# Hybrid RWKV-7 and sparse-attention block on one core: order of the Gram products, layout of the Gram matrices in DRAM, place of the first branch's weight split

## Chip, cores and metric

One core of one Trainium2 chip. The metric is the device time of one execution in microseconds; the time before is the median of three runs. TensorE is PE here (PEld: its weight loads), VectorE DVE, ScalarE ACT, GpSimd POOL, SyncE SP, as in the profile.

## The reference

The kernel computes one block of a model for a sequence of 2048 positions and width 1024. What matters for the change, cut to its core:

```python
p = h @ w_in[l]                       # h: rms_norm(x), scaled and shifted; then a token shift on some columns
(pr, pk, pv, pwd, pad_, z_a, q, ckv, z_b, qi, ki, wi, g_a, g_b) = jnp.split(p, split_at, axis=-1)
y_a = rwkv7_branch(pr, pk, pv, pwd, pad_, ...)      # 8 heads of 64, a scan over the sequence:
#   sa    = einsum('bhvk,bhk->bhv', state, a_t)
#   state = state * w_t + sa b_t + v_t k_t ;  y_t = einsum('bhvk,bhk->bhv', state, r_t)
y_b = dsa_branch(q, ckv, qi, ki, wi, ...)           # 256 keys chosen for each query, softmax over them
br_a = (y_a * jax.nn.silu(z_a)) @ w_pa[l]
br_b = (y_b * jax.nn.silu(z_b)) @ w_pb[l]
merged = jax.nn.sigmoid(g_a) * br_a + jax.nn.sigmoid(g_b) * br_b
x = x + gate * (merged @ w_o[l])
```

## The kernel before, in words

The sequence is cut into four blocks of 512 positions (`tb`, NTB = 4), and the block's stages are written one after the other in `build`. A scheduler orders the instructions of each engine by a priority that `band(p)` sets (a lower number comes first) and by what each instruction waits for; so stages with different bands run beside each other. Tiles come from pools, and a pool opened where an older one lay waits for the last readers of the older one's tiles. fp32 numbers that need full precision are split into a high and a low part, and a product is three matmuls: high-high, high-low, low-high.

1. Selection of keys (to about 800 us), then the projection `h @ w_in` in pieces: `gemm_half` (matmuls at L251, weights loaded at L230 into `wraw`, split into `whi` and `wlo` on ACT and POOL). For z and g, one unit of 128 rows is copied from PSUM into a tile `eo` (L347) and stored to DRAM (L349). The last piece is `gemm_half((2, 3), ("z", "g"))` at band 70000, which ends near 1694 us.
2. Beside the projection, the scan in a chunked form, for each `tb`. `rwkv_pass` (L612) builds, for each of four pairs of heads `p` and 8 chunks `c`, products of `bk` and `ar`, both 128 rows: two heads of 64. Its Gram products (L703) take rows 0 to 63 or 64 to 127 (`hh`) of `bk` and `ar`, 128 x 128 each, four chunks to a PSUM tile `pg`; DVE multiplies the tile with a mask into `gt` (L705), and a DMA stores it to `gmd` (L706). `rwkv_inv` (L722) loads the 32 x 32 diagonal blocks of the stored matrices as `ln` (L730), with one (chunk, head) matrix to a partition, and inverts the triangular matrices by 31 pairs of DVE instructions (`prd` L740, `tm` L742). `rwkv_chain` (L749) goes through the chunks in order: it loads `gmc` (L762), and its matmuls (L777, L782, L788, L791, L797, L801, L808) depend on each other and on the chunk before.
3. `branch_a` (L1122), at band 75000: `split_weights` (L1007) loads the four row blocks of w_pa, casts the high part on ACT (L1019) and subtracts the low part on DVE and POOL in turn (L1020). Then, for 8 steps of 256 positions (`fb`), `gated` (L1024) loads z and y (`zy`, L1057 and L1058; one buffer for y) in two halves and makes `uh`, `ul` of y silu(z) on POOL (L1043), DVE (L1049) and ACT (L1050); `branch` (L1099) does the matmuls (L1111), loads g (L1114), takes its sigmoid, multiplies, and the result goes back to DRAM.
4. Attention (from 1817 us) and the finish (from 2250 us) with the second branch and w_o.

All DMAs below are issued by SP, in the order in which they stand on its queue; an issue whose data isn't ready holds up what stands behind it.

Of the kernel before, what the change touches and what calls it, by code (L numbers as in the profile page):

```python
# [24 lines left out]
FT = mybir.dt.float32  # L25
# [4 lines left out]
OP = mybir.AluOpType  # L30
AX = mybir.AxisListType.X
PSUM = bass.MemoryType.PSUM
# [5 lines left out]
NTB = S // TB  # L38
# [3 lines left out]
FB = 256  # L42
# [9 lines left out]
class Block:  # L52
# [479 lines left out]
    def rwkv_open(self, ctx):  # L532
        nc, x = self.nc, self.x
        V, A, G, DMA = nc.vector, nc.scalar, nc.gpsimd, nc.sync
        R = self.R = {}
# [55 lines left out]
        for i in range(2):  # L591
            h = c1.tile([128, 4, 128], FT, name=f"H{i}")
# [1 line left out]
            R["H"].append(h)  # L594
        R["n"], R["late"] = 0, []
        d = self.d
        R["gm"] = [d.tile([8, 128, 8, 128], FT, name=f"gmd{i}") for i in range(NTB)]
        R["ar"] = [d.tile([8, 128, 4, 128], FT, name=f"ard{i}") for i in range(NTB)]
        R["bk"] = [d.tile([8, 128, 512], FT, name=f"bkd{i}") for i in range(NTB)]
        R["vt"] = [d.tile([512, 512], FT, name=f"vtd{i}") for i in range(NTB)]  # L600
# [11 lines left out]
    def rwkv_pass(self, tb):  # L612
        nc, R = self.nc, self.R
        V, A, T, G, DMA = nc.vector, nc.scalar, nc.tensor, nc.gpsimd, nc.sync
        ld, wk, st, ps = R["ld"], R["wk"], R["st"], R["ps"]
        P = self.PJ[tb]
        gm4 = R["k_gm"][:, None, :].to_broadcast([128, 4, 128])

        def pg(shape=(128, 512)):
            return ps.tile(list(shape), FT, name="pg")  # L620
# [23 lines left out]
        for p in range(4):  # L644
# [10 lines left out]
            u = wk.tile([128, 512], FT, name="u")  # L655
# [40 lines left out]
            G.tensor_copy(wl, e65[:, :, 64])  # L696
            DMA.dma_start(self.WL[tb][p], wl)
            for c0 in (0, 4):
                for hh in range(2):
                    r_ = slice(hh * 64, hh * 64 + 64)  # L700
                    pt = pg((128, 4, 128))
                    for j in range(4):
                        T.matmul(pt[:, j], bk[r_, c0 + j, :], ar[r_, c0 + j, :], start=True, stop=True)  # L703
                    gt = st.tile([128, 4, 128], FT, name="gt", bufs=4)
                    V.tensor_tensor(gt, pt, gm4, op=OP.mult)  # L705
                    DMA.dma_start(R["gm"][tb][c0:c0 + 4, :, 2 * p + hh, :].rearrange("c q t -> q c t"), gt)  # L706
            G.tensor_tensor(bk, bk, e65[:, :, 64:65].to_broadcast([128, 8, 128]), op=OP.mult)
            for c0 in (0, 4):
                pt = pg((128, 4, 128))
# [12 lines left out]
    def rwkv_inv(self, tb):  # L722

        nc, R = self.nc, self.R
        V, G, DMA = nc.vector, nc.gpsimd, nc.sync
        st = R["iv"]
        ln = st.tile([128, 32, 32], FT, name="ln", bufs=1)
        for b in range(2):
            for c in range(8):
                DMA.dma_start(ln[b * 64 + c * 8:b * 64 + c * 8 + 8],  # L730
                              R["gm"][tb][c, b * 32:b * 32 + 32, :, b * 32:b * 32 + 32].rearrange("s h t -> h s t"))
        tm = st.tile([128, 32, 32], FT, name="tm", bufs=1)
        G.memset(tm, 0.0)
        G.memset(tm.rearrange("p a b -> p (a b)")[:, ::33], 1.0)
        prd = st.tile([128, 1024], FT, name="prd", bufs=1)

        for s in range(31):
            r, n = 31 - s, s + 1
            v = prd[:, :r * n].rearrange("p (t j) -> p t j", t=r)
            V.tensor_tensor(v, ln[:, s, n:][:, :, None].to_broadcast([128, r, n]),  # L740
                            tm[:, s, 0:n][:, None, :].to_broadcast([128, r, n]), op=OP.mult)
            V.tensor_tensor(tm[:, n:, 0:n], tm[:, n:, 0:n], v, op=OP.add)  # L742
        tt = ln
        V.tensor_copy(tt.rearrange("p s t -> p t s"), tm)
        DMA.dma_start(R["ti"][tb], tm[0:64])
        DMA.dma_start(R["tt"][tb][0], tt[0:64])
        DMA.dma_start(R["tt"][tb][1], tt[64:128])

    def rwkv_chain(self, tb):  # L749
        nc, R = self.nc, self.R  # L750
# [7 lines left out]
        for c in range(8):  # L758
            arc = ch.tile([128, 4, 128], FT, name="arc")
            DMA.dma_start(arc, R["ar"][tb][c])  # L760
            gmc = ch.tile([128, 8, 128], FT, name="gmc")
            DMA.dma_start(gmc, R["gm"][tb][c])  # L762
            bkc = ch.tile([128, 512], FT, name="bkc")
            DMA.dma_start(bkc, R["bk"][tb][c])
            uv = ch.tile([128, 512], FT, name="uv")
# [353 lines left out]
    def rows(self, t, k, qs):  # L1119
        return t[k * 128:(k + 2) * 128, qs].rearrange("(k p) t -> p k t", p=128)  # L1120

    def branch_a(self, fbs):  # L1122

        nc = self.nc
        with ExitStack() as ctx:
            k1 = self.pool("ba1", 1, ctx=ctx)
            w = self.pool("baw", 2, side="right", ctx=ctx)
            ps = self.pool("bap", 2, PSUM, ctx=ctx)
            W = {}
            self.split_weights(W, k1, w, (("w_pa", 4),), (nc.vector, nc.gpsimd))  # L1130
            self.ba = []
            for fb in fbs:
                tb, qs = fb // 2, slice((fb % 2) * FB, (fb % 2) * FB + FB)
                u = self.gated(w, ps, fb, 0)
                for m in range(0, 8, 2):
                    g = self.branch(w, ps, fb, 0, m, W["w_pa"], u)
                    self.ba.append(nc.sync.dma_start(self.rows(self.GG[tb], m, qs), g))

    def finish(self):
        nc, tc, x = self.nc, self.tc, self.x  # L1140
# [66 lines left out]
    def build(self, upto="all"):  # L1207
# [65 lines left out]
        hctx.close()  # L1273
        R["ictx"].close()
        R["qctx"].close()
        self.band(70000)
        self.gemm_half((2, 3), ("z", "g"))
        gctx.close()
        k = self.pool("late")
        self.lsum = k.tile([128, NQB, 8], FT, name="lsum")  # L1280
        done = range(S // FB)
        self.ubufs = 2
        self.gbufs = 8
        self.pbufs = 2
        self.ybufs = 1
        self.band(75000)
        actx = ExitStack()
        self.hd0 = self.pool("ath0", 1, ctx=actx)
        self.branch_a(done)
        rctx.close()  # L1290
        self.fiA = self.pool("fia", 1, ctx=actx)
        self.fiW = self.pool("fiw0", 1, ctx=actx)
# [84 lines left out]
```

## Time and profile before

| | before |
|---|---|
| median of 3 runs | 2542.9 us (2539.11 to 2544.07) |
| profiled execution, own time | 2535.82 us |
| its span | 2534.0 us |
| PE busy | 2414.3 us (95%) |
| DVE, ACT, POOL busy | 1615.2 (64%), 1235.3 (49%), 804.8 (32%) us |
| DMA traffic | 415.67 MB, mean 164 GB/s |

The span runs from the first to the last instruction of the profiled execution. Times of the rows below count from its start. Matmuls are pipelined: the rows give the length of one from its start to its modelled end, and the next may start earlier. fp32 matmuls that are not split (the Gram products and the chain) stand as two records each, so a row with x8 is four matmuls.

### The profile page before, as it was taken

What the parts mean: (1) busy time and instruction counts of PE and PEld (TensorE: products, weight loads), DVE (VectorE), ACT (ScalarE), POOL (GpSimd) and SP (SyncE); (2) the same over time, 40 slices, a digit from 0 to 9 for tenths busy, and PEclk for the clock granted to TensorE, in tenths of its full rate; (3) what the DMA queues carried; (4) which work ended last, traced back from release to release, by engine and by line L of the source; (5) the groups of instructions that cost most, each with busy time, mean ns of one, the idle gap of its engine ahead of it and who ended that gap; (6) DMA issues with size and microseconds to landing.
All of it is one profiled execution on the core that took longest, in us unless ns stands there. A gap on an engine that the chain in (4) does not pass through costs nothing.

```text
span 2534.0 us, 44949 instructions
## 1 busy us (share of the span) xinstructions
PE 2414.3 (95%) x16776; PEld 2134.6 (84%) x16776; DVE 1615.2 (64%) x3381; ACT 1235.3 (49%) x2024; POOL 804.8 (32%) x694
## 2 busy tenths in 40 slices
PE   4899999999999999999999999999889999989998
PEld 3687878888888998889888989989779999988887
DVE  6614778776877556654936757344478888876443
ACT  4414646555544424334434333352478888865332
POOL 2411111111121333233333332131255555544332
PEclk9999999999999999999999999999999999999999
DMA  7754223423336556777677769978753343155442
GB/s 248 280 152 125 89 83 92 125 96 96 104 98 217 147 164 193 191 203 225 194 206 212 214 188 276 298 240 250 232 166 87 91 118 99 29 182 192 142 150 71
DMA packets 423496, 415.67 MB, mean 164 GB/s; under 512 B 80010, under 2 KB 339890, under 8 KB 418404
## 3 DMA queue, kind: packets, MB, share of 16 engines
q1 hardware_dynamic: 422692, 404.33, 53.1%
q0 software_dynamic: 576, 8.39, 0.8%
q8 instruction: 132, 2.16, 0.4%
q14 instruction: 96, 0.79, 0.1%
HBM read 254.04 MB, written 160.15 MB: 163 GB/s over the span
## 4 chain that ended last, share of the span: by engine, by line
PE 49%; DMA 7%; DVE 5%; issue 3%; ACT 2%; SPq 2%; POOL 2%; POOLq 0%; ACTq 0%; DVEq 0%
PE g L251 16%; PE fo L1196 6%; PE yv L993 4%; PE br L1111 4%; PE pt L976 3%; PE pg L703 2%; PE lg L959 2%; PE lg L960 2%; DMA xt<-in_w_pb_dram 1%; PE pp L808 1%; PE pp L791 1%; PE zu L797 1%; PE hp L801 1%; PE pp L788 1%; DVE prd L740 1%
## 5 line engine op out<-in xcount | busy, mean ns | idle before, releaser
L251 PE MATMUL g<-hh,whi 128*128 128x256 f32 (+1 forms) x2176 | 718.9, 330 | 8.8 <-DVE eo L265 4.7
L251 PE MATMUL g<-hl,whi 128*128 128x256 f32 (+1 forms) x2176 | 715.3, 329 | 2.9 <-POOL hl L169 2.9
L251 PE MATMUL g<-hh,wlo 128*128 128x256 f32 (+1 forms) x2176 | 714.9, 329 | 1.4 <-POOL wlo L237 1.4
L237 POOL TENSOR_TENSOR wlo<-wraw,whi 128x1024 fp32r<-128x1024 f32 (+1 forms) x89 | 225.1, 2529 | 748.3 <-ACT whi L236 695.0
L251 PEld LDWEIGHTS g<-hh,whi 128*128 128x128 f32 x2176 | 416.0, 191 | 54.7 <-issue 6.5
L251 PEld LDWEIGHTS g<-hl,whi 128*128 128x128 f32 x2176 | 416.2, 191 | 43.4 <-issue 4.1
L251 PEld LDWEIGHTS g<-hh,wlo 128*128 128x128 f32 x2176 | 416.0, 191 | 41.7 <-issue 4.3
L431 DVE SCALAR_TENSOR_TENSOR sc<-re,wi,sc 128x1024 f32<-128x1024 f32 (+7 forms) x154 | 170.7, 1108 | 56.7 <-ACT re L425 50.8
L425 ACT ACTIVATE re<-ixs 128x1024 f32<-128x1024 f32 (+7 forms) x176 | 140.4, 816 | 135.5 <-PE ixs L423 78.7
L236 ACT CAST whi<-wraw 128x1024 fp32r<-128x1024 f32 (+1 forms) x89 | 92.8, 1043 | 174.2 <-PE g L251 132.3
L976 PE MATMUL pt<-ident,lt 128*128 128x128 f32 x1088 | 168.1, 275 | 7.0 <-ACT tp L982 4.3
L966 ACT ACTIVATE lt<-lt,nm 128x128 f32<-128x128 f32 (+15 forms) x128 | 154.8, 1212 | 15.3 <-DVE nm L965 15.2
L987 DVE TENSOR_TENSOR pl<-pt,ph 128x512 fp32r<-128x512 f32 (+1 forms) x216 | 139.0, 657 | 31.6 <-ACT ph L986 30.7
L423 PE MATMUL ixs<-kim,st 128*128 128x512 f32 (+3 forms) x608 | 150.2, 373 | 8.3 <-ACT re L425 4.8
L962 DVE CUSTOM_DVE_ANT_0 lt<-lg,mask 128x512 f32<-128x512 f32 (+3 forms) x256 | 147.4, 589 | 16.5 <-PE lg L960 9.0
L993 PE MATMUL yv<-ph,vp 128*128 128x256 f32 (+1 forms) x576 | 152.1, 285 | 5.7 <-ACT ph L986 5.6
L993 PE MATMUL yv<-pl,vp 128*128 128x256 f32 x576 | 153.0, 301 | 2.0 <-POOL pl L984 1.8
L959 PE MATMUL lg<-m,sq 128*128 128x256 f32 (+3 forms) x384 | 136.6, 365 | 5.9 <-DMA mask<-mask 4.1
L423 PEld LDWEIGHTS ixs<-kim,st 128*128 128x128 f32 x608 | 113.1, 190 | 34.5 <-ACT re L425 6.9
L976 PEld LDWEIGHTS pt<-ident,lt 128*128 128x128 f32 x1088 | 125.7, 141 | 16.9 <-ACT tp L982 5.3
L986 ACT CAST ph<-pt 128x512 fp32r<-128x512 f32 (+1 forms) x216 | 116.4, 564 | 20.8 <-PE pt L976 14.3
L960 PE MATMUL lg<-m,sq 128*128 128x256 f32 (+3 forms) x384 | 126.2, 336 | 0.0
(343 smaller groups left out, 5106.6 us busy)
## 6 DMA issues: line engine op xcount, KB each, us to landing
wraw<-in_w_in_dram SPq DMA_DIRECT2D x88, 512.0 KB
gg<-eo SPq DMA_DIRECT2D x64, 256.0 KB
gmd<-gt SPq DMA_DIRECT2D x64, 256.0 KB
gmc<-gmd SPq DMA_DIRECT2D x32, 512.0 KB
g<-gg SPq DMA_DIRECT2D x64, 256.0 KB
m<-ks SPq DMA_DIRECT2D x32, 512.0 KB
pj<-eo SPq DMA_DIRECT2D x52, 256.0 KB
x<-in_ada_w_dram SPq DMA_DIRECT2D x24, 512.0 KB
```

The costliest lines, as they stand in the source:

```text
L237: nc.gpsimd.tensor_tensor(lo[:, :, :n], raw[:, :, :n], hi[:, :, :n].bitcast(FT), op=OP.subtract)
L251: T.matmul(p[:, s], a[:, k], b[:, k, s], start=n == 0, stop=n == 3 * KD - 1)
L423: T.matmul(p[:, a:b], st[:, h], M[i][:, k0 + a:k0 + b], start=i == 0, stop=i == 1)
L425: A.activation(r[:, :kn], p[:, :kn], AF.Relu)
L431: V.scalar_tensor_tensor(o, r[:, :kn], wi, o, op0=OP.mult, op1=OP.add)
L959: T.matmul(p[:, :kn], sq[:, qb * 128:(qb + 1) * 128], m1[:, k0:k1_], start=True, stop=False)
L960: T.matmul(p[:, :kn], sq[:, qb * 128:(qb + 1) * 128], m2[:, k0:k1_], start=False, stop=True)
L962: V.tensor_tensor_reduce(lt[:, k0:k1_], p[:, :kn], mk, 1.0, -3.0e38, OP.subtract, OP.max, cm[:, i:i + 1])
L966: ex = A.activation(lt[:, :n], lt[:, :n], AF.Exp, bias=nm, accum_out=lsum[:, qb, h:h + 1])
L976: T.transpose(p[:, o:o + 128], L[i][:, kt * 128:(kt + 1) * 128], self.ident)
L993: T.matmul(yv[:, qs], vp[:, kt, :], b[:, o:o + nn], start=kt == 0 and i == 0, stop=kt == last and i == 1, skip_group_check=True)
L1196: T.matmul(p, a[:, k, q], b[:, k, s], start=n == 0, stop=n == 23)
```

## The change

Three things, and the title's last words ("output tiles stay in a bank of their own, passes at 2 tiles") say what is as before.

- In `rwkv_pass`, the two PSUM tiles of the halves are taken together, and the products are written alternating, half 0 and half 1 of chunk `j`, then of `j + 1`; the two evictions and stores follow.
- The Gram matrices lie in DRAM by row: [row, chunk, head, column] in place of [chunk, row, head, column]. A store writes four chunks of a head; `rwkv_inv` loads its blocks by 2 DMAs of 64 partitions in place of 16 of 8; `rwkv_chain` reads `[:, c]`.
- `branch_a` is cut in two. `branch_open` opens the pools of w_pa (`ba1`), of its raw tiles (`bas`) and of the branch's PSUM (`bap`), all on the right side, and splits w_pa; it stands ahead of the last projection piece in `build`, at band 72000. `branch_a` opens the pool for u, z, y and g (`baw`) after the projection and goes through the steps.

```diff
-        R["gm"] = [d.tile([8, 128, 8, 128], FT, name=f"gmd{i}") for i in range(NTB)]
+        R["gm"] = [d.tile([128, 8, 8, 128], FT, name=f"gmd{i}") for i in range(NTB)]
...
             for c0 in (0, 4):
+                pts = [pg((128, 4, 128)) for hh in range(2)]
+                for j in range(4):
+                    for hh in range(2):
+                        r_ = slice(hh * 64, hh * 64 + 64)
+                        T.matmul(pts[hh][:, j], bk[r_, c0 + j, :], ar[r_, c0 + j, :], start=True, stop=True)
                 for hh in range(2):
-                    r_ = slice(hh * 64, hh * 64 + 64)
-                    pt = pg((128, 4, 128))
-                    for j in range(4):
-                        T.matmul(pt[:, j], bk[r_, c0 + j, :], ar[r_, c0 + j, :], start=True, stop=True)
                     gt = st.tile([128, 4, 128], FT, name="gt", bufs=4)
-                    V.tensor_tensor(gt, pt, gm4, op=OP.mult)
-                    DMA.dma_start(R["gm"][tb][c0:c0 + 4, :, 2 * p + hh, :].rearrange("c q t -> q c t"), gt)
+                    V.tensor_tensor(gt, pts[hh], gm4, op=OP.mult)
+                    DMA.dma_start(R["gm"][tb][:, c0:c0 + 4, 2 * p + hh, :], gt)
...
         for b in range(2):
-            for c in range(8):
-                DMA.dma_start(ln[b * 64 + c * 8:b * 64 + c * 8 + 8],
-                              R["gm"][tb][c, b * 32:b * 32 + 32, :, b * 32:b * 32 + 32].rearrange("s h t -> h s t"))
+            b_ = slice(b * 32, b * 32 + 32)
+            DMA.dma_start(ln[b * 64:b * 64 + 64], R["gm"][tb][b_, :, :, b_].rearrange("s c h t -> (c h) s t"))
...
-            DMA.dma_start(gmc, R["gm"][tb][c])
+            DMA.dma_start(gmc, R["gm"][tb][:, c])
...
-    def branch_a(self, fbs):
+    def branch_open(self, ctx):
         nc = self.nc
-        with ExitStack() as ctx:
-            k1 = self.pool("ba1", 1, ctx=ctx)
-            w = self.pool("baw", 2, side="right", ctx=ctx)
-            ps = self.pool("bap", 2, PSUM, ctx=ctx)
-            W = {}
-            self.split_weights(W, k1, w, (("w_pa", 4),), (nc.vector, nc.gpsimd))
...
+        k1 = self.pool("ba1", 1, side="right", ctx=ctx)
+        w = self.pool("bas", 2, side="right", ctx=ctx)
+        ps = self.pool("bap", 2, PSUM, side="right", ctx=ctx)
+        W = {}
+        self.split_weights(W, k1, w, (("w_pa", 4),), (nc.vector, nc.gpsimd))
+        return ps, W["w_pa"]
+
+    def branch_a(self, fbs, ctx, ps, wt):
+        nc = self.nc
+        w = self.pool("baw", 2, side="right", ctx=ctx)
...
+        bctx = ExitStack()
+        self.band(72000)
+        ba = self.branch_open(bctx)
         self.band(70000)
         self.gemm_half((2, 3), ("z", "g"))
...
-        self.branch_a(done)
+        self.branch_a(done, bctx, *ba)
+        bctx.close()
```

What the scheduler makes of it, at three places. A row of the built order gives line, operation, output<-inputs with the number of the buffer, size, and how many alike follow each other.

PE, Gram products of a head pair in one of the passes, among matmuls of the chain (L782 to L791) and of the projection (L251). Before, `pg_13751`, `13759`, `13767` and `13775` are the four tiles of this pair; the second and the third stand next to each other:

```order
L703 MATMUL pg_13751<-ar_13728,bk_13729 128x128 x4
L782 MATMUL zu_14280<-ttc_14264,t1c_14265 32x32 x4
L690 MATMUL pg_13737<-ei_13739,blk_8649 128x512
L782 MATMUL zu_14280<-ttc_14264,t1c_14265 32x32 x4
L788 MATMUL pp_14290<-H0_8664,arc_14256 128x128 x4
L791 MATMUL pp_14290<-uv_14262,gmc_14258 64x64 x6
L703 MATMUL pg_13759<-ar_13728,bk_13729 128x128 x4
L703 MATMUL pg_13767<-ar_13728,bk_13729 128x128 x4
L791 MATMUL pp_14290<-uv_14262,gmc_14258 64x64 x2
```
With the change `pg_13709` and `13710` are the two halves of the first four chunks, `13725` and `13726` those of the others:

```order
L704 MATMUL pg_13709<-ar_13686,bk_13687 128x128 x4
L783 MATMUL zu_14224<-ttc_14208,t1c_14209 32x32 x4
L690 MATMUL pg_13695<-ei_13697,blk_8649 128x512
L783 MATMUL zu_14224<-ttc_14208,t1c_14209 32x32 x4
L789 MATMUL pp_14234<-H0_8664,arc_14200 128x128 x4
L792 MATMUL pp_14234<-uv_14206,gmc_14202 64x64 x6
L704 MATMUL pg_13710<-ar_13686,bk_13687 128x128 x4
L704 MATMUL pg_13725<-ar_13686,bk_13687 128x128 x4
L792 MATMUL pp_14234<-uv_14206,gmc_14202 64x64 x2
```
Each tile's four products still stand in one row, and the two halves of the first four chunks are apart by other work. Over the whole program a row of four of one half and a row of four of the other make a run of eight 8 times now, 7 before.

SP, loads for the first inversion (`ln`), behind the chain's first `gmc`. Before:

```order
L762 DMA gmc_9860<-gmd0_8668 128x1024
L762 DMA gmc_9939<-gmd0_8668 128x1024
L730 DMA ln_9188<-gmd0_8668 8x32x32 x8
L714 DMA bkd0_8676<-gt_9169 128x4x128
L75 DMA lat3_76<-eo_15479 128x512
L714 DMA bkd0_8676<-gt_9177 128x4x128
...
L720 DMA vtd0_8680<-gt_9185 128x4x128
L730 DMA ln_9188<-gmd0_8668 8x32x32 x6
...
L730 DMA ln_9188<-gmd0_8668 8x32x32 x2
L633 DMA pk_9312<-pj1_69 128x512
```
With the change:

```order
L763 DMA gmc_9832<-gmd0_8668 128x1024
L763 DMA gmc_9911<-gmd0_8668 128x1024
L732 DMA ln_9188<-gmd0_8668 64x32x32 x2
L716 DMA bkd0_8676<-gt_9169 128x4x128
L75 DMA lat3_76<-eo_15423 128x512
L716 DMA bkd0_8676<-gt_9177 128x4x128
```
The 16 loads stood in three rows, with stores and loads of other stages between; now both stand in the first row's place.

SP, end of the last projection piece. `gg2`, `gg3` <- `eo` are the stores of its units; `z`, `y`, `g` the loads of the branch's first step. Before, from the fifth-last of these stores on:

```order
L349 DMA gg3_84<-eo_18712 128x512
L1018 DMA xt_18956<-in_w_pa_dram 128x1024
L1018 DMA xt_18960<-in_w_pa_dram 128x1024
L1057 DMA z_18974<-z0_77 128x2x256
L764 DMA bkc_15061<-bkd3_8679 128x512
L762 DMA gmc_15059<-gmd3_8671 128x1024
L766 DMA uv_15063<-vtd3_8683 64x512
L1058 DMA y_18976<-ya0_101 128x2x256
L1057 DMA z_18984<-z0_77 128x2x256
L1114 DMA g_19019<-gg0_81 128x2x256
L849 DMA bo_15135<-bod3_8687 128x2x256
L1114 DMA g_19049<-gg0_81 128x2x256
```
With the change:

```order
L349 DMA gg2_83<-eo_18851 128x512
L349 DMA gg3_84<-eo_18903 128x512
L1058 DMA z_18921<-z0_77 128x2x256
L1059 DMA y_18923<-ya0_101 128x2x256
L1058 DMA z_18931<-z0_77 128x2x256
L1115 DMA g_18966<-gg0_81 128x2x256
L1115 DMA g_18996<-gg0_81 128x2x256
...
L1059 DMA y_18933<-ya0_101 128x2x256
L1115 DMA g_19198<-gg0_81 128x2x256
```
The loads of z, y and g stood among the projection's stores; now the first of them stands directly behind the last two stores, and the second y behind seven loads of g.

## Rows read from the trace of the kernel before

**Rows 1.** The page's first part: busy time (share of the span), instructions.
```profile
PE 2414.3 (95%) x16776; PEld 2134.6 (84%) x16776; DVE 1615.2 (64%) x3381; ACT 1235.3 (49%) x2024; POOL 804.8 (32%) x694
```

**Rows 2.** Busy table: stretch, length, PE, PEld, DVE, ACT, POOL, PEclk, DMA share, GB/s.
```profile
1100.00:1694.00 594.00, 592.56 (x5775) 538.22 (x5775) 334.70 (x604) 226.08 (x383) 183.75 (x180) 1.00 0.78 230
1694.00:1713.00 19.00, 15.88 (x174) 14.37 (x172) 9.95 (x10) 9.28 (x15) 9.90 (x6) 0.91 0.49 145
1740.00:1780.00 40.00, 33.52 (x262) 32.55 (x261) 11.96 (x18) 10.16 (x18) 5.12 (x4) 0.96 1.03 314
1780.00:1817.00 37.00, 34.31 (x280) 33.50 (x281) 13.99 (x21) 10.54 (x19) 5.16 (x4) 1.00 0.59 191
```

**Rows 3.** The same table, beside the first inversion.
```profile
1030.00:1090.00 60.00, 52.09 (x384) 47.71 (x383) 46.88 (x85) 15.39 (x23) 14.01 (x8) 0.94 0.61 162
1083.00:1090.00 7.00, 5.93 (x23) 5.06 (x24) 2.57 (x7) 0.49 (x1) 0.00 (x0) 0.51 0.66 168
```

**Rows 4.** Timeline of PE, Gram matmuls: start, us, engine, line, operation, out<-in, count.
```profile
898.09 1.16 PE L703 MATMUL pg<-ar,bk 64*128 64x128 f32 x8
...
903.29 1.71 PE L703 MATMUL pg<-ar,bk 64*128 64x128 f32 x16
```

**Rows 5.** Timeline of SP's queue, loads of the first inversion.
```profile
1011.44 6.57 SPq L730 DMA_DIRECT2D ln<-gmd  x8
...
1032.22 0.88 SPq L730 DMA_DIRECT2D ln<-gmd  x2
```

**Rows 6.** Timeline of DVE, inversion 0; idle before <-releaser in brackets.
```profile
1037.94 0.19 DVE L740 TENSOR_TENSOR prd<-ln,tm 128x31 f32<-128x31 f32 x1 [5.69 <-DMA pk<-pj]
...
1084.40 0.19 DVE L742 TENSOR_TENSOR tm<-tm,prd 128x31 f32<-128x31 f32 x1
```

**Rows 7.** Timeline of PE around the end of the projection.
```profile
1693.60 0.69 PE L782 MATMUL zu<-ttc,t1c 32*32 32x32 f32 x16
...
1697.76 1.11 PE L797 MATMUL zu<-xx,ttc 64*64 64x64 f32 x16 [1.32 <-issue]
...
1701.03 0.58 PE L1111 MATMUL br<-uh,w_pal 128*128 128x256 f32 x1 [1.28 <-DVE w_pal L1020]
...
1712.10 0.39 PE L1111 MATMUL br<-uh,w_pal 128*128 128x256 f32 x1 [0.37 <-POOL w_pal L1020]
```

**Rows 8.** Groups of instructions, 1693 to 1817 us: the split of w_pa.
```profile
L1020 POOL TENSOR_TENSOR w_pal<-xt,w_pah 128x1024 fp32r<-128x1024 f32 x2 | 5.6, 2788 | 0.2
L1019 ACT CAST w_pah<-xt 128x1024 fp32r<-128x1024 f32 x4 | 4.1, 1044 | 1.9 <-DMA xt<-in_w_pa_dram 1.5 <-DMA gg<-eo 0.3
L1020 DVE TENSOR_TENSOR w_pal<-xt,w_pah 128x1024 fp32r<-128x1024 f32 x2 | 3.2, 1606 | 3.0 <-ACT w_pah L1019 3.0
```

**Rows 9.** Timeline of SP's queue: loads of the first branch.
```profile
1658.84 0.59 SPq L1058 DMA_DIRECT2D y<-ya  x1
1659.47 0.48 SPq L1057 DMA_DIRECT2D z<-z  x1
```

**Rows 10.** Chain that ended last, 1690 to 1720 us: start, us, what.
```profile
1691.20 2.48 PE g L251 x19
...
1693.70 0.59 ACT eo L347
...
1694.31 3.50 DMA gg<-eo
...
1718.36 2.75 DMA g<-gg
```

**Rows 11.** Instruction groups y, z (1693 to 1817 us) and uh (1640 to 1800).
```profile
L1043 POOL TENSOR_TENSOR y<-z,y 128x512 f32<-128x512 f32 x12 | 15.7, 1304 | 86.2 <-DMA y<-ya 46.2 <-DMA z<-z 33.1 <-DVE ul L1051 3.5
...
L1049 DVE TENSOR_TENSOR z<-y,sz 128x512 f32<-128x512 f32 x13 | 10.8, 834 | 30.7 <-POOL y L1043 30.7
...
L1050 ACT CAST uh<-z x15: 601/617/622, 1669.2 to 1799.2; 128x512 fp32r<-128x512 f32 x15
```

**Rows 12.** Timeline of PE, a stop inside the branch.
```profile
1747.93 0.39 PE L1111 MATMUL br<-uh,w_pah 128*128 128x256 f32 x1 [3.92 <-DVE g L1116]
```

More of the change, by code (lines that the diff above doesn't have):

```diff
@@ L1120, in rows @@
         return t[k * 128:(k + 2) * 128, qs].rearrange("(k p) t -> p k t", p=128)
-    def branch_a(self, fbs):
+    def branch_open(self, ctx):
         nc = self.nc
-        with ExitStack() as ctx:
-            k1 = self.pool("ba1", 1, ctx=ctx)
-            w = self.pool("baw", 2, side="right", ctx=ctx)
-            ps = self.pool("bap", 2, PSUM, ctx=ctx)
-            W = {}
-            self.split_weights(W, k1, w, (("w_pa", 4),), (nc.vector, nc.gpsimd))
[L1131 to L1137, printed above, removed]
+        k1 = self.pool("ba1", 1, side="right", ctx=ctx)
[7 more added lines that the diff above has]
+        w = self.pool("baw", 2, side="right", ctx=ctx)
+        self.ba = []
+        for fb in fbs:
+            tb, qs = fb // 2, slice((fb % 2) * FB, (fb % 2) * FB + FB)
+            u = self.gated(w, ps, fb, 0)
+            for m in range(0, 8, 2):
+                g = self.branch(w, ps, fb, 0, m, wt, u)
+                self.ba.append(nc.sync.dma_start(self.rows(self.GG[tb], m, qs), g))
     def finish(self):
@@ L1275, in build @@
         R["qctx"].close()
+        self.ubufs = 2
+        self.gbufs = 8
+        self.pbufs = 2
+        bctx = ExitStack()
+        self.band(72000)
+        ba = self.branch_open(bctx)
         self.band(70000)
@@ L1281, in build @@
         done = range(S // FB)
-        self.ubufs = 2
-        self.gbufs = 8
-        self.pbufs = 2
         self.ybufs = 1
```

## The prediction

> **What bounds the kernel now.** I read the page's busy table first: TensorE is busy 95% of the span, so only what shortens its queue of matmuls, or what it stands idle for, can move the end [rows 1]. The table of stretches then says where it stands idle [rows 2]. From 1100 to 1694 us it is busy 592.56 us of 594.00: there a gain on another engine is worth nothing. There are three stretches that the change touches in which it is not full: 1030 to 1090 us, beside the first inversion; 1694 to 1713 us, where the projection ends and the first branch starts; and 1740 to 1780 us, inside the branch, with the DMA engines at a share of 1.03. In the first the loss is 60.00 - 52.09 = 7.9 us of idle time, and the granted clock is 0.51 over 1083 to 1090 us, the lower of its two levels, which costs about half of 7.00, 3.4 us: 11.3 us together [rows 3]. In the second it is 19.00 - 15.88 = 3.1 us, and the clock is 0.91. Last I read single rows around the three places: TensorE's timeline, SyncE's DMA issues, the chain that ended last.
>
> **Gram products: 0 us.** Each of the 64 groups of four products is 8 records. A group alone takes 1.16 us; two groups of opposite row halves back to back take 1.71 us, not 2.3 [rows 4]: where a product of the upper rows stands next to one of the lower rows, they share time. The rule that speaks of this is in the Trainium skill, "TensorE: Matmul & The Clock Gate", Part 3, on packing small matmuls by row and column tiling: matmuls with few rows that lie in distinct row groups of the array run concurrently. By it the source order of the change (half 0, half 1, half 0, ...) would hide half of all these products; the 1.71 us agree with it. But by the built order the four products of one tile still stand together: almost every row of that table is x4 on one tile, and the two halves are neighbours about as often as before (8 runs of eight against 7). What the source alternates, the order sets back into fours. If full alternation came about, 64 groups would lose half of 1.16 us each where they aren't paired already, 28 us with the 7 or 8 pairs taken off; as the order stands I take 0, -1 to +1.
>
> **Loads of the inversion: -4 us.** Before, 16 DMAs of 8 partitions fetch the blocks. SyncE issues the first 8 from 1011.44 for 6.57 us and the last two at 1032.22 [rows 5]; behind these stands pk. VectorE starts the first product pair at 1037.94, having waited 5.69 us, by the row for pk, and ends the last at 1084.40 [rows 6]: so 46 us of VectorE work, mixed with that of a pass, run through just the stretch in which TensorE loses 11.3 us [rows 3]. With the change one row of two DMAs stands where the first eight stood, and nothing of it is left behind the lat, qs and bkc rows. If two DMAs with as many pieces take what 16 took on SyncE, twice 6.57 = 13.1 us, they end at about 1024.6, and the pairs could start 13 us earlier, into time in which VectorE waits (the 5.69 us among it). Bounds: all 11.3 us gone would be -10 with what remains of the clock, and the pairs only taking the place of the pass's own VectorE work would be up to +4. I take -4, since the pairs' 46 us don't shrink, and the pass's own evictions still wait in the same VectorE queue. The three later inversions lie where TensorE is full (592.56 of 594.00): 0, whichever way. The gmd stores and gmc loads keep their 512-byte and 4-KB pieces; I take 0 for them, under the same cover.
>
> **w_pa split, moved ahead: -3.4 us.** Before, the first cast waits behind the last eo copies on ScalarE, and TensorE stops for the low parts twice, 1.28 us at 1701.03 and 0.37 at 1712.10 [rows 7]; with the clock at 0.91 over 19 us, another 1.7 [rows 2]. Sum -3.35. The work itself is 4 casts of 1.04, 2 VectorE subtractions of 1.6 and 2 GpSimd ones of 2.8 us [rows 8], now beside the last projection, where those engines are not full. Were a cast to stand before an eo copy and wait for its weights, the copy and its g tile would be late: +2 at most. Nothing of the chain late either: -5.
>
> **What the change adds: a wait for z and y at the end of the projection, +10.4 us.** Before, the branch's pool lies on space that is free early: SyncE issues the first y at 1658.84 and the second z at 1659.47 [rows 9], and the first u is cast at 1669.2 [rows 11], 24 us before the last projection matmul ends at 1693.7, where the copy of its tile starts [rows 10]. With w_pa's tiles opened first, that pool comes to lie on the projection's own wlo and eo tiles. The built order shows it: every z, y and g load stands behind the last two gg stores. From T0, the end of the last projection matmul, the chain of waits has in its own rows: eo copy 0.59, store 3.50 to landing, a load of as much as one of these (128x2x256 numbers, 256 KB) 2.75 [rows 10], then GpSimd y 1.30, VectorE z 0.83, ScalarE uh 0.62 [rows 11]; with 0.5 us for two issues that is T0+10.1 for the first branch matmul. Meanwhile TensorE has only the chain's last chunk, six rows from 0.69 us, as at 1693.60, to 1.1, as at 1697.76, 6.0 us in all, with two exposed waits of 1.3 us, as the one of 1.32 there [rows 7]: it ends at T0+8.6, 1.5 us idle. 14 branch matmuls (1.8 us, by 2.48 us for 19 of the same shape [rows 10]) later the second half of u is needed. Its y has one buffer, free at about T0+8.8, and its load stands behind seven g loads: u at about T0+16, 4.2 us idle. Two more windows of the lower clock, as the one after the pause at 1701, cost 1.7 each. Idle and clock 2.6 + 1.5 + 4.2 + 3.4 = 11.7, of which 1.3 is there before: +10.4. Bounds: +3 (the store and the load overlap with the chain's last chunk, the clock holds) to +14 (the seven g loads, 1.8 MB, hold y up by another 4 us).
>
> **The branch without its lead: +4 us.** Each of 8 steps moves 12 DMAs of 256 KB for 96 matmuls. Before, it enters with two u ready and all g loaded, and still stops 3.92 us at 1747.93 [rows 12], with the DMA share at 1.03 [rows 2], while attention's first loads run. With no u in hand each late load shows. Bounds 0 and +10; I take +4, one more stop like that one.
>
> **Sum.** 0 - 4 - 3.4 + 10.4 + 4 = +7.0 us. The profiled execution took 2535.8 us and becomes 2542.8. It stands 7.1 us under the median of the three runs, 2542.9, against which the change is timed: **2550 us** (2549.9 rounded). A difference under 0.2%, 5 us, can't be told from none.
>
> **Rivals.**
> - *The inversion's early start pays in full, faster.* Pairs that start 13 us sooner take all 11.3 us of [rows 3] away, w_pa 3.4, and the switch costs 6 (one clock window, y behind fewer g loads): -8.7, 2534 us. It decides if the pairs come ahead of the pass's evictions, that is if they begin before about 1026. For it: VectorE waits then. Against it: the 46 us of pairs. 0.25.
> - *Nothing to be told.* The switch costs 8, with no lost lead, and the inversion and w_pa give 7 to 8: 2543 us. For it: the branch's DMA share is only 0.59 from 1780 on [rows 2], so a lead can be made up. 0.30.
> - *DMA pile-up.* All 12 loads of the first step (3 MB) come at once behind T0 and meet attention's first loads: the whole +10 of the lost lead and +13.5 at the switch, less 3.5: +20, 2562 us. 0.11.
> - *Halves overlap after all*, as the alternation says it does: -28, 2515 us. The price is from [rows 4], against it stands the built order. 0.03. The Trainium skill's "TensorE: Matmul & The Clock Gate", Part 3, has this as its rule.
> - My forecast: 2550 us, its own range 2548 to 2556. 0.31.
>
> **Numbers.** Under 2537.8 lie the first and the fourth rival: 0.28 faster. The second is 0.30 same. Forecast and pile-up: 0.42 slower. The range is 2533 to 2563: it leaves out the far half of the first rival, the fourth, and the pile-up's far end, some 0.19.
>
> **What would show it.** Gram rows of x8 at 1.16 us, few x16. One row of ln loads near 1011 us, the pairs' start before 1030, and fewer than 11.3 us lost in the 60 us around it. No wait for w_pal. SyncE's first z and y after the last gg store, GpSimd's y waiting for them, TensorE idle 8 to 9 us in the 20 after T0, at the lower clock for one to three windows. I am wrong if z and y are issued some 30 us before T0 still, if the x16 rows come to the most, or if TensorE is full from T0 on.

## The result, and the profile after

| | before | after |
|---|---|---|
| median | 2542.74 us (4 runs) | 2560.15 us (4 runs, 2557.59 to 2561.9) |
| ratio | | 1.0067, 95% interval 1.0045 to 1.0089 |
| span of the profiled execution | 2534.0 us | 2555.8 us |

The change costs 17.4 us by the medians. (Between the two profiled executions it is 21.8 us: that of before lies 6.9 us under its median, that of after 2.6 us.) The prediction said 2550, slower, with a range to 2563. TensorE has the same share, 95%, and is busy 14.2 us longer [rows 1]:

```profile
PE 2428.5 (95%) x16776; PEld 2148.6 (84%) x16776; DVE 1619.7 (63%) x3381; ACT 1233.7 (48%) x2022; POOL 805.6 (32%) x694
```
The busy table of the kernel after (columns as in [rows 2]): beside the first inversion, beside the second, beside the fourth, a piece behind the last projection matmul, and the whole stretch from there to the first matmul of attention.

```profile
1030.00:1090.00 60.00, 57.23 (x497) 53.17 (x496) 50.93 (x91) 19.78 (x31) 21.26 (x16) 1.00 0.72 195
1240.00:1270.00 30.00, 26.69 (x214) 24.66 (x215) 17.21 (x28) 10.30 (x16) 8.14 (x8) 0.89 0.65 173
1583.00:1593.00 10.00, 8.08 (x54) 7.21 (x52) 2.55 (x5) 2.42 (x5) 0.00 (x0) 0.66 1.05 292
1708.60:1729.10 20.50, 13.86 (x64) 12.25 (x65) 10.29 (x19) 13.91 (x21) 4.27 (x4) 0.50 0.70 227
1703.80:1836.50 132.70, 112.20 (x856) 108.19 (x855) 49.66 (x78) 44.79 (x73) 20.55 (x16) 0.88 0.75 231
```
And the row of before for that whole stretch:

```profile
1693.70:1816.45 122.75, 110.47 (x953) 106.98 (x952) 51.58 (x78) 40.71 (x66) 22.76 (x16) 0.97 0.73 226
```
Beside the first inversion only 60.00 - 57.23 = 2.8 us are idle, at the full clock, where 7.9 were [rows 3]; beside the second and the fourth, where TensorE was full, it now stands 3.3 and 1.9 us and the clock is 0.89 and 0.66. The last stretch takes 132.7 us instead of 122.75 and holds fewer matmul records, 856 instead of 953: a chunk of the scan's chain (96 records, some 6.5 us of TensorE in seven rows of 0.7 to 1.2) has come to stand ahead of the projection's end. That end, T0 from here on, comes 10.1 us later (1703.8, 1693.7).

Timeline of PE, rows that answer to [rows 4, 7]: two Gram rows, the waits for the second and the fourth inversion, and the first branch matmuls of the two halves of u.

```profile
899.32 1.16 PE L704 MATMUL pg<-ar,bk 64*128 64x128 f32 x8
...
904.52 1.71 PE L704 MATMUL pg<-ar,bk 64*128 64x128 f32 x16
...
1255.39 1.06 PE L778 MATMUL zu<-t1c,gmc 32*32 32x32 f32 x16 [3.31 <-DMA t1c<-tid]
...
1585.72 1.06 PE L778 MATMUL zu<-t1c,gmc 32*32 32x32 f32 x16 [1.92 <-DMA t1c<-tid]
...
1714.56 0.80 PE L1112 MATMUL br<-uh,w_pah 128*128 128x256 f32 x2 [1.42 <-ACT uh L1051]
...
1722.29 0.80 PE L1112 MATMUL br<-uh,w_pah 128*128 128x256 f32 x2 [4.38 <-ACT uh L1051]
```
Gram rows are as before: x8 in 1.16 us, x16 in 1.71. Timeline of SP's queue, to [rows 5, 9]:

```profile
1013.07 4.32 SPq L732 DMA_DIRECT2D ln<-gmd  x2
...
1694.65 10.11 SPq L349 DMA_DIRECT2D gg<-eo  x2
1706.58 0.37 SPq L1058 DMA_DIRECT2D z<-z  x1
1707.00 0.46 SPq L1059 DMA_DIRECT2D y<-ya  x1
...
1708.02 4.90 SPq L1115 DMA_DIRECT2D g<-gg  x7
1713.88 0.36 SPq L1059 DMA_DIRECT2D y<-ya  x1
```
The ln loads are two DMAs of 4.32 us together. The z, y and g loads come behind the last gg store, for whose tile SP waits from 1694.65 on. DVE and POOL, to [rows 6, 11]: the first instruction of the first inversion, and the first four y products of the branch.

```profile
1021.99 0.19 DVE L741 TENSOR_TENSOR prd<-ln,tm 128x31 f32<-128x31 f32 x1 [3.76 <-DMA ln<-gmd]
```
```profile
1711.86 1.27 POOL L1044 TENSOR_TENSOR y<-z,y 128x512 f32<-128x512 f32 x1 [9.48 <-DMA y<-ya]
1718.83 1.27 POOL L1044 TENSOR_TENSOR y<-z,y 128x512 f32<-128x512 f32 x1 [5.70 <-DMA y<-ya]
1723.85 1.28 POOL L1044 TENSOR_TENSOR y<-z,y 128x512 f32<-128x512 f32 x1 [3.74 <-DMA y<-ya]
1728.65 1.29 POOL L1044 TENSOR_TENSOR y<-z,y 128x512 f32<-128x512 f32 x1 [3.53 <-DMA y<-ya]
```
The waits of PE between the projection and attention, to [rows 12]: engine, line, awaited, us, times, longest.

```profile
PE br L1112 <- ACT uh L1051: 9.6, 3, 4.4
PE br L1112 <- DVE g L1117: 8.2, 5, 2.9
```

### The profile page after: what moved, and what is told of

Its sections match the earlier page's. It is cut to its first block, busy times and chain, and to the rows that moved or that the text cites. A ratio compares the mean times of both kernels' runs of the same rounds, so it can differ in the third digit from the quotient of the medians.

```text
span 2555.8 us, 44911 instructions
## 1 busy us (share of the span) xinstructions
PE 2428.5 (95%) x16776; PEld 2148.6 (84%) x16776; DVE 1619.7 (63%) x3381; ACT 1233.7 (48%) x2022; POOL 805.6 (32%) x694
## 4 chain that ended last, share of the span: by engine, by line
PE 47%; DMA 7%; DVE 6%; issue 3%; ACT 2%; POOL 1%; SPq 1%; POOLq 0%; ACTq 0%; DVEq 0%
PE g L251 13%; PE fo L1202 5%; PE yv L994 4%; PE br L1112 4%; PE pt L977 3%; PE pg L704 2%; PE lg L960 2%; PE lg L961 2%; PE pp L809 1%; PE zu L798 1%; PE pp L792 1%; PE pp L789 1%; DMA xt<-in_w_pb_dram 1%; PE hp L802 1%; DMA g<-gg 1%
## 5 line engine op out<-in xcount | busy, mean ns | idle before, releaser
L251 PE MATMUL g<-hh,whi 128*128 128x256 f32 (+1 forms) x2176 | 719.0, 330 | 4.0 <-DVE prev L339 3.1
L251 PE MATMUL g<-hl,whi 128*128 128x256 f32 (+1 forms) x2176 | 717.6, 330 | 2.9 <-POOL hl L169 2.8
L251 PE MATMUL g<-hh,wlo 128*128 128x256 f32 (+1 forms) x2176 | 715.1, 329 | 1.7 <-POOL wlo L237 1.7
L251 PEld LDWEIGHTS g<-hh,whi 128*128 128x128 f32 x2176 | 417.4, 192 | 47.2 <-issue 5.5
L251 PEld LDWEIGHTS g<-hl,whi 128*128 128x128 f32 x2176 | 417.3, 192 | 44.1 <-POOL hl L169 3.7
L251 PEld LDWEIGHTS g<-hh,wlo 128*128 128x128 f32 x2176 | 417.2, 192 | 41.3 <-issue 4.4
L987 ACT CAST ph<-pt 128x512 fp32r<-128x512 f32 (+1 forms) x216 | 116.1, 564 | 20.9 <-PE pt L977 14.5
```

Source lines behind the costliest of these rows:

```text
L251: T.matmul(p[:, s], a[:, k], b[:, k, s], start=n == 0, stop=n == 3 * KD - 1)
```

## The experiments

Each ratio is to the kernel before, run beside it on the same chip; its medians there were 2540.3 (e1 to e4), 2542.9 (e5 to e8) and 2540.8 us (e9 to e12). "The stretch" is that from the last projection matmul to the first matmul of attention, 122.75 us before and 132.70 after, in one execution of each. T0 itself can't be compared to better than several us between two executions: TensorE's order is the same in e9 and in the changed kernel up to 1722 us, and T0 is 9.3 us apart, most of it from 834 to 869 us.

| run | median us | ratio, 95% interval | the stretch us, its PE records |
|---|---|---|---|
| e1 alternating alone | 2547.5 | 1.0032 (1.0019 to 1.0045) | 126.00, 857 |
| e2 layout alone | 2549.4 | 1.0034 (1.0017 to 1.0051) | 122.70, 856 |
| e11 both of them | 2551.7 | 1.0042 (1.0027 to 1.0056) | 123.10, 856 |
| e3 split ahead alone | 2552.6 | 1.0043 (1.0027 to 1.0058) | 136.30, 953 |
| e4 change, first u ahead | 2544.1 | 1.0015 (1.0001 to 1.0028) | 126.20, 858 |
| e5 alternation forced | 2561.4 | 1.0086 (1.0068 to 1.0103) | 174.80, 1364 |
| e6 chunk ahead | 2552.6 | 1.0046 (1.0032 to 1.0060) | 125.30, 896 |
| e7 split and first u ahead | 2540.5 | 0.9996 (0.9985 to 1.0007) | 127.30, 954 |
| e8 busy in the wait | 2561.5 | 1.0082 (1.0067 to 1.0097) | 132.90, 909 |
| e9 change, two y | 2550.3 | 1.0028 (1.0015 to 1.0041) | 120.00, 858 |
| e10 e7 with two y | 2525.7 | 0.9937 (0.9918 to 0.9957) | 113.30, 953 |
| e12 before, two y | 2536.0 | 0.9976 (0.9965 to 0.9986) | 118.70, 952 |

**The parts alone.** e1 has the first part of the diff (products alternating), e2 the second (layout, ln and gmc loads), e11 both, e3 the third (the split ahead, `baw` behind).

> Only the Gram products written alternating, all else as before. Theory A (the order sets them back into fours, nothing moves): within 5 us of the kernel before, 2538 to 2548 us, and nearly all Gram rows x8 at 1.16 us, some 8 of x16 at 1.71. Rival (both tiles taken together hold the pass up): 5 to 10 us slower, with waits for gt before the Gram products. Rival (halves overlap): 20 to 28 us faster.

> Only the Gram matrices by row and the two ln loads. Theory A (the first inversion starts 16 us earlier and TensorE gains 10 to 12 us there, but inversions 1 and 3 make it wait as in the changed kernel, 5 to 7 us each): within 5 us of before. Rival (the waits at inversions 1 and 3 have to do with the other parts): 8 to 12 us faster. Rival (the layout is what costs the 17 us): 10 to 17 us slower.

The two are slower by much the same, and neither by the expected way: theory A said within 5 us for both. (e1 has the number of its first rival, 5 to 10 us, but not its waits: the Gram products wait 0.9 us for gt in e1 as before.) In both the projection ends about 8 to 10 us later (1701.8 and 1703.3) with the chain one chunk further, and the stretch behind it is no shorter without that chunk. Waits of PE in e1, 1701.8 to 1730 us, and the stretch of both:

```profile
PE br L1112 <- ACT w_pah L1020: 2.3, 2, 1.3
PE br L1112 <- POOL w_pal L1021: 1.5, 1, 1.5
PE br L1112 <- DVE w_pal L1021: 0.9, 2, 0.5
```
```profile
1701.80:1827.80 126.00, 107.28 (x857) 103.27 (x856) 45.95 (x71) 36.71 (x58) 17.89 (x13) 0.95 0.67 210
```
```profile
1703.30:1826.00 122.70, 107.41 (x856) 103.80 (x854) 45.97 (x71) 36.72 (x58) 18.94 (x13) 0.94 0.68 216
```
The waits for the w_pa split, 1.28 and 0.37 us before [rows 7], are 4.7 us in e1 (2.7 in e2): the chunk that stood among the first branch matmuls had covered them. In e2 the waits beside the second and fourth inversions are there as in the changed kernel (3.32 us at 1258, 1.85 at 1588), so they belong to the layout.

> The change without its third part: Gram products alternating and the layout by row, the branch as before. Theory (both alone move the same chunk of the chain ahead of the projection's end, so the loss is had once): 6 to 11 us slower than before. Rival (each part has a loss of its own): 14 to 18 us slower.

As the theory had it, the loss is had once: 0.42%, not 0.66%.

**The chunk by itself.** e6 is the kernel before with one ordering edge:

```diff
+                mark = T.matmul(pp[0:64, ...], gmc[64:128, h, 0:64], uv[64:128, ...], ...)   # chain of tb 3, c == 6
...
+                    if kind == "g" and i == 15 and tb == 3:
+                        with self.tc.issue_after(self.R["mark"].ins):
+                            p = self.unit(wt, tb)
```

> The kernel before, with one ordering edge: the last projection unit's matmuls stand behind the seventh chunk's products with uv in the last chain, so that one chunk of the chain instead of two is left behind the projection, as in the runs with the alternation alone and the layout alone. Nothing else differs. Theory A (those runs were slower because that chunk no longer covers the waits for the w_pa split, and the phase behind the projection does not get shorter without it): 5 to 10 us slower than before. Rival (the place of the chunk is worth nothing, the loss was in the new loads and tiles): within 3 us of before.

It is slower by 0.46%, at least as much as e1 and e2, and waits for the same split, 4.6 us. So chain work that moves ahead of the projection's end is enough for a loss of that size. That isn't all that e6's trace shows: only 57 records leave the stretch, and from attention's first matmul to the last matmul it takes 713.8 us, 707.8 before, which is open. Waits of PE from 1702 to 1732 us, and the stretch:

```profile
PE br L1117 <- ACT w_pah L1025: 2.4, 1, 2.4
PE br L1117 <- POOL w_pal L1026: 2.2, 2, 1.2
```
```profile
1702.00:1827.30 125.30, 109.69 (x896) 105.76 (x894) 49.35 (x74) 38.39 (x61) 21.88 (x16) 0.95 0.68 215
```
**The wait for z and y.**

> Only the split of w_pa ahead of the last projection piece, with the pool of z, y, g and u opened behind it. Theory A (the wait for z and y at the end of the projection, and the lower clock behind it, are the whole of the loss): 14 to 20 us slower than before, first branch matmul 10 to 11 us after the last projection matmul, TensorE at the lower clock for 15 to 25 us there. Rival (the loss needs the other parts too): within 6 us of before.

Slower by 0.43%, 11 to 12 us, between the two and nearer to theory A. The first branch matmul comes 11.65 us after the projection's end, and the stretch is 13.5 us longer than before with the same records:

```profile
1695.50:1831.80 136.30, 120.44 (x953) 116.11 (x951) 51.15 (x82) 46.71 (x78) 21.78 (x18) 0.90 0.72 227
```
e4 gives the first step a pool of its own (14 KB for each partition) beside the w_pa split:

```diff
+        w0 = self.pool("ba0", 1, side="right", ctx=ctx)
+        self.ubufs = self.ybufs = 1
+        self.u0 = self.gated(w0, ps, 0, 0)
...
-            u = self.gated(w, ps, fb, 0)
+            u = self.gated(w, ps, fb, 0) if fb else self.u0
```

> The changed kernel, but z, y and u of the first step in a pool of their own of 14 KB that lies on free space, loaded beside the projection; g and all later steps as in the changed kernel. Theory A (the late z and y of the first step are the cause): TensorE goes on with the branch at once, no wait over 2 us and at most one window of the lower clock in the 30 us behind the last projection matmul; 10 to 16 us faster than the changed kernel, 2544 to 2551 us. Rival (the loads of the later steps and of g, all late, pile up on the DMA engines whatever the first step has): the stop moves to the second step, under 5 us gained, 2555 us or more.

TensorE goes on with the branch at once, and 13 us of the 17 come back. But the stops move on, as the rival had it in part: 2.73, 2.64 and 6.33 us at 1724.66, 1762.59 and 1775.31, and only 6.5 us of the gain lie in the stretch. Behind it e4 is 9.2 us shorter (700.3 us from attention's first matmul to the last matmul, against 709.5), all of it in attention's first 130 us. There a wait of the changed kernel is gone:

```profile
PE lg L960 <- DMA mask<-mask: 4.0, 1, 4.0
```
SyncE issues the mask 2.3 us behind attention's first matmul in the changed kernel and 0.8 us ahead of it in e4; what makes up the rest is open. e7 is the same on the kernel before (e3 with the first u ahead):

> Gram products and layout as before, the w_pa split ahead, and the first step's z, y and u in a pool of their own ahead too. Theory A (late z and y, and one chunk less of cover, are the two causes): two chunks lie behind the projection again and the first u is there, 0 to 8 us faster than before. Rival (the loads of the second and later steps, all late, cost as much as the split gains): 2 to 8 us slower, as the changed kernel with the first u ahead.

The same time as before, at the far end of what theory A expected: neither of the two causes is left, and the stretch is still 4.5 us longer than before. So something else has a part in its length.

**The clock.** e8 is the changed kernel with matmuls into a PSUM tile that nobody reads:

```diff
+        for i in range(12):
+            nc.tensor.matmul(self.dm[:, 0:256], self.dw[:, 0, 0:128], self.dw[:, 0, 0:256], start=True, stop=True)
...
+                if not br and not fb and not m and not i and k == 1:
+                    with self.tc.issue_after(mm.ins):
+                        for q in range(40): ...    # the same matmul
```

> The changed kernel with 12 idle matmuls ahead of the first branch matmul and 40 behind the seventh, of 0.12 us each, which nobody reads: TensorE is busy in the two waits behind the projection. z, y and g come as late as in the changed kernel. Theory A (about half of the loss there is the lower clock that follows the waits): under 8 us at the lower clock in the 30 us behind the projection, where it was 20.5 us, and 5 to 10 us faster than the changed kernel. Rival (the clock falls all the same, or the loads alone set the pace): within 3 us of it.

The rival is right on the time, theory A on the clock. Timeline of PE in e8; busy table of the 30 us behind T0 in the changed kernel, then in e8, and of e8's stretch; e8's waits of PE in the stretch:

```profile
1708.47 1.69 PE L1145 MATMUL dm<-w_pah 128*128 128x256 f32 x12
...
1716.95 0.79 PE L1112 MATMUL br<-uh,w_pah 128*128 128x256 f32 x2 [2.71 <-ACT uh L1051]
...
1718.91 5.99 PE L1117 MATMUL dm<-w_pah 128*128 128x256 f32 x34
```
```profile
1703.80:1733.80 30.00, 22.38 (x159) 20.29 (x159) 13.40 (x23) 16.59 (x26) 5.26 (x5) 0.66 0.66 212
1705.80:1735.80 30.00, 25.64 (x219) 24.34 (x217) 12.31 (x22) 15.93 (x26) 5.15 (x4) 0.89 0.63 199
1705.80:1838.70 132.90, 116.30 (x909) 113.07 (x907) 49.06 (x78) 44.56 (x73) 20.71 (x16) 0.92 0.75 231
```
```profile
PE br L1112 <- DVE g L1121: 11.7, 6, 4.0
PE br L1112 <- ACT uh L1051: 3.0, 2, 2.7
```
Over the 30 us the granted clock is 0.89, where it was 0.66, with 20.50 us of it at the lower level. Yet the stretch is as long, 132.90 us. The idle matmuls stand in the two waits for u, and what the clock saves behind them comes back as waits for g: 11.7 us, where they were 8.2. (br's PSUM tile comes free when DVE has multiplied it with the sigmoid of g.)

**The stream of u.** In the changed kernel POOL's y products follow each other every 4.8 us at the least (1718.83, 1723.85, 1728.65): y load, POOL, DVE, and only then the next y load, as y has one buffer. Until then SyncE stands at the y load, and the loads of z and g behind it stand too. Waits of SyncE for this in the stretch, in the changed kernel, then in e9:

```profile
SPq L1059 <- DVE z L1050: 12.1, 10, 3.2
SPq L1059 <- DVE z L1050: 7.9, 9, 2.3
```
The stretch is 8.1 us to the first of the 16 y products, 107.5 from there to the last, and 17.2 behind it. Seven of the 15 intervals are 4.8 to 5.6 us; the others are 7 to 14.3, the longest where attention's loads come. 16 times 5.0, 80 us, is thus a floor and not the length. e9, e10 and e12 give y and the sigmoid two buffers each (which of the two counts isn't told apart), an edit of one number in the changed kernel, in e7 and in the kernel before:

```diff
-        self.ybufs = 1
+        self.ybufs = 2
         self.band(75000)
```

> The changed kernel with two buffers each for y and silu's sigmoid in the first branch (4 KB more for each partition), so that the load of a half's y need not wait until VectorE has read the half before. Theory B (behind the projection the time is set by the stream of u, one half after the other through a single y buffer, 5.0 us at the least, and not by TensorE or its clock): the stretch from the last projection matmul to the first attention matmul falls from 132.7 us to 118 to 125, and the time by 8 to 15 us, to 2545 to 2552. Rival (the loads are slow because the DMA engines are full there): under 4 us.

> Two buffers for y, with w_pa split ahead, the first u ahead, and Gram products and layout as before. Theory B: 3 to 12 us faster than the kernel before, 2530 to 2539 us. Rival (the DMA engines set the pace): as without the second buffer, 2538 to 2543 us.

> The kernel before with two buffers for y and the sigmoid in the first branch. Theory B (the stream of u sets the phase there too, though two steps are ready when it begins): 2 to 8 us faster than before. Rival (with its lead, before is bound by TensorE and the w_pa split): within 2 us.

All three moved as theory B said, e10 by more. The first y products of e9, in pairs now, e9's waits of PE in the stretch, and the stretch of e9, e10 and e12:

```profile
1720.04 1.27 POOL L1044 TENSOR_TENSOR y<-z,y 128x512 f32<-128x512 f32 x1 [8.32 <-DMA z<-z]
1723.48 1.28 POOL L1044 TENSOR_TENSOR y<-z,y 128x512 f32<-128x512 f32 x1 [2.17 <-DMA y<-ya]
1730.85 1.29 POOL L1044 TENSOR_TENSOR y<-z,y 128x512 f32<-128x512 f32 x1 [6.10 <-DMA z<-z]
1732.90 1.53 POOL L1044 TENSOR_TENSOR y<-z,y 128x512 f32<-128x512 f32 x1 [0.76 <-DMA z<-z]
```
```profile
PE br L1112 <- DVE g L1117: 7.2, 5, 2.7
PE br L1112 <- ACT uh L1051: 1.4, 1, 1.4
```
```profile
1713.10:1833.10 120.00, 107.76 (x858) 104.87 (x856) 51.90 (x78) 44.97 (x73) 21.05 (x16) 0.93 0.80 256
```
```profile
1698.70:1812.00 113.30, 108.39 (x953) 106.26 (x951) 51.28 (x78) 43.11 (x72) 20.78 (x17) 0.98 0.83 262
```
```profile
1696.50:1815.20 118.70, 109.29 (x952) 106.85 (x951) 51.13 (x77) 40.56 (x64) 21.12 (x15) 0.96 0.73 227
```
In e9 the first and the last y product are 93.3 us apart, not 107.5, and the waits for u fall from 9.6 to 1.4 us; those for g hardly change (8.2 and 7.2), though in e10 they are 4.1 us where e7 has 8.7. e10 is 0.63% faster than the kernel before, and faster than both kernels of this study: with two y, a w_pa that is ready and the first u ahead, the stretch falls to 113.30 us. The split and the first u ahead are worth nothing with one y (e7, 0.9996) and 0.39% with two (e10 against e12), which is the plainest sign that the one buffer held their gain back.

Not all of the stretch goes by that buffer. In its middle, beside attention's first loads, the DMA engines are full, before (1.03 over 40 us [rows 2]) as after (0.97 over 35 us; 0.99 in e9, 1757 to 1792 us):

```profile
1755.00:1790.00 35.00, 29.20 (x229) 28.80 (x229) 11.46 (x18) 7.31 (x12) 5.16 (x4) 0.95 0.97 290
```
**Overlap of the Gram halves.** e5 holds the order by an edge from each product to the next:

```diff
+                        with self.tc.issue_after(prev.ins):
+                            prev = T.matmul(pts[hh][:, j], bk[r_, c0 + j, :], ar[r_, c0 + j, :], start=True, stop=True)
```

> The kernel before, with the eight Gram products of a head pair held in the order half 0, half 1, half 0, ... by an ordering edge from each to the next, so that the scheduler cannot set them back into fours. Theory A (the halves overlap only where neighbours in the order are of different halves): neighbours start under 10 ns apart, a run of seven products takes about 1.1 us where two runs of four took 2.3, TensorE's Gram work falls by 25 to 30 us, and the time by 15 to 28 us. Rival (no overlap for pairs of single products, or the waits for two free tiles eat it): within 5 us of before.

The first half of theory A holds, the second does not. Timeline of PE: a wait, and seven products in a row; then the stretch:

```profile
1006.80 0.79 PE L690 MATMUL pg<-kk,blk 128*128 128x512 f32 x1 [7.29 <-ACT kk L608]
...
1126.00 1.16 PE L708 MATMUL pg<-ar,bk 64*128 64x128 f32 x14
```
```profile
1666.90:1841.70 174.80, 155.77 (x1364) 146.21 (x1362) 73.41 (x119) 62.97 (x107) 33.21 (x32) 0.89 0.80 251
```
14 records take 1.16 us, as long as 8 did. From each record's start to the next one's, all 512 take 49.1 us, against 65.3 before: 16 us saved, not 25 to 30, since the second record of a pair of different halves starts 6 to 8 ns after the first, but the next pair only 105 ns later, and each group's first product stands alone. (The Trainium skill, "TensorE: Matmul & The Clock Gate", Part 3, has matmuls of distinct row groups run concurrently; the 6 to 8 ns agree.) But TensorE waits 7.29 us for ACT's kk at 1006.80 (why ACT comes late there isn't shown), and the chain falls back: its first product in each of the four blocks comes 1.9, 14.5, 27.9 and 38.8 us later than before. Four more chunks of it are left behind a projection that ends 26.8 us sooner (1364 records in the stretch). The whole is 0.86% slower.

## Why the prediction was right, and where it was not

The sign, the place and the mechanism that was priced highest were right; the sum was 10 us short. 2560 lies in the stated range, but outside the forecast's own, 2548 to 2556, and beside the pile-up's 2562: the range was wide enough to hold two parts of the sum that were too low by 7.4 and 5.5 us. In the two traces, ahead of T0 the sum had -4 and the rows give +3.4 beside the chunk that moved (8.5 gained at the first inversion, 11.9 lost at the second and the fourth, clock included; with the chunk's 6.5 that is about the 10.1 us of T0). Behind T0 the sum had +11.0, for the split, the wait and the lead. The stretch is 10.0 us longer with the chunk gone from it, so some 16.5 on equal work; e3, with as many records there as before, has 13.5.

- **Gram products, 0 (-1 to +1).** Right for the products: still fours, x8 in 1.16 us, and 65.6 us for all 512 records by the same count that gave 65.3. Wrong as a bound: the edit also moved other rows of the order, and alone costs 0.32% (e1). The rows of the built order that the prediction went by were those of the products alone.
- **Loads of the inversion, -4.** The pairs start at 1021.99, 16 us earlier, and the first inversion's place gives more than was taken: 5.1 us of idle time and the clock, near the "pays in full" rival. The 0 for the three later inversions, "whichever way", was the step that failed: TensorE's order had followed the earlier inversion. The chain's first products of the second and the fourth block now stand 13.2 and 7.7 us earlier than before (1255.39 and 1585.72, against 1268.6 and 1593.4), where the stored inverse is not yet back (3.31 and 1.92 us, and 6.7 us by the clock). That the place was full before showed that nothing was waited for in the old order, and said nothing on a new one.
- **w_pa split, -3.4.** The waits for w_pal are gone, as said. The time that they gave did not come through, since u and g come no sooner (e7 and e10 show it for the split, e8 for the clock).
- **Wait for z and y, +10.4.** The chain of waits came as written: z issued 2.8 us after the projection's end (4.4 had been taken, by the store's 3.50), first branch matmul at T0+10.8 (10.1), second half at T0+18.5 (16), idle 1.42 and 4.38 us (1.5 and 4.2) with two waits of 0.8 in the chain. The clock was undersized: 20.50 us at the lower level, 10 us lost where 3.4 were taken; but by e8 the clock's part should not have been added at all while the loads set the pace.
- **Lost lead, +4.** Undersized, and the cause of the rest. It was taken as one more stop; the runs show that the single y buffer sets the pace of u where the DMA engines aren't full. That it also holds back g, behind it in SyncE's queue, shows in e10 and hardly in e9. The kernel before has that buffer too (e12 gains 0.24%), but begins the stretch two steps ahead. With two y the changed kernel's stretch is 12.7 us shorter (e9).
- **Not in the sum:** the chunk of the chain that moved ahead of the projection's end. By e6 its place alone costs 0.46% with one y. It isn't additive to the rest: the first two parts cost 0.42% (e11), the third 0.43% (e3), all three 0.67%. What they share is the stretch: work that leaves it uncovers waits and doesn't shorten it.

The pile-up rival named 2562 us, close to the result; its mechanism is there only in part. (Its 12 loads are four of z and y and eight of g, two steps' worth of g.) The DMA engines are full for 35 us beside attention's first loads, but before as well. Over the whole stretch the share is 0.75, and one more buffer gives 10 us back. It remains open what, beside the mask, makes attention's first 130 us shorter in e4, and what sets the waits for g that stay with two y. The wait for the second inverse is the way through DRAM: SyncE issues the store at 1248.57, 0.03 us after VectorE's last product, and the chain goes on at 1255.39. Whether that way can be shortened was not tried.

## What to carry to other kernels

Before pricing stops one by one in a stretch, ask which stream sets its length: follow one buffer around (load, use, free, load) and multiply its period by the turns. That is a floor (80 us of 132.7 here); what else shares the queue or fills the DMA engines comes on top, and the test is one more buffer. Idle time and a low clock inside such a stretch can be slack, and then are not to be summed (e8). Work that is taken out of a stretch with such a bound, or moved ahead of it, gave nothing there (e2: 122.70 us with 97 records fewer) and may have been the cover of its other waits. And an edit that a scheduler undoes at its own place may still move rows elsewhere: compare where long chains stand in the order, not only the edited rows.

## What was not expected of the hardware

Matmuls of the two row halves start 6 to 8 ns apart when they alternate, and 16 us of TensorE time can be had so, but only where the order truly alternates. Idle matmuls did raise the granted clock behind the projection (0.89 over 30 us, against 0.66), and the kernel was not faster for it.
